# One level of Strassen's algorithm in a float32 feed-forward layer

## The chip, the core and the metric

The kernel runs on one core of one Trainium2 chip. The metric is device time in microseconds (us), from the first to the last instruction of one launch; the median of three runs before the change is 1940.48 us (1940.22 to 1940.63). The core's engines run side by side, each through its own list of instructions, and wait for each other by semaphores: TensorE (PE) multiplies, VectorE (DVE) and ScalarE (ACT) work on elements, GpSimd (POOL) does some of that and issues a few transfers, SyncE (SP) issues most transfers.

## The reference, cut to what matters

Everything is float32, with 512 tokens, a model width of 2048 and a feed-forward width of 5632:

```python
x = x + jnp.concatenate([y_f, y_g], axis=-1) @ w_out[l]      # the mixers, then the output projection
h2 = rmsnorm(x, norm_ffn[l])
x = x + (jax.nn.silu(h2 @ w_gate[l]) * (h2 @ w_up[l])) @ w_down[l]
return rmsnorm(x, norm_final)
```

The three products of the second half are what the change touches: `h2 @ w_gate` and `h2 @ w_up` (512 x 2048 times 2048 x 5632), and the down projection (512 x 5632 times 5632 x 2048).

## The kernel before, in words

**Split products.** A float32 operand is carried as two float32r tiles, hi (leading 12 bits) and lo (the rest), and a product is three matmuls: hi·hi, hi·lo and lo·hi, accumulated in PSUM (`mm3`, lines 82 to 84). Weights come from memory in units of 128 x 1024 (512 KB). ACT makes hi by a cast (line 76), DVE makes lo by a subtraction (line 77). There are three buffers each for raw, hi and lo, so a unit can be made ready while the two before it are in use.

**Stages.** Input projection and mixers (0 to about 303 us of the trace), output projection (to 485 us), feed-forward (to the end). In the output projection, four column blocks of 512 are computed one after the other; behind each block DVE adds the residual (line 459), ACT sums the squares (line 453), and PE transposes the 16 tiles of the block (line 444), from which ACT and DVE make hi and lo of the next product's operand (lines 447, 448). The norm's 1/rms by token isn't needed for that: it is applied later to the products (`ffn_scales`, lines 493 and 497).

**Feed-forward.** `gate_up(f)` computes one tile of 128 of the 5632 features, for all 512 tokens: 16 contraction tiles x 3 matmuls with 512 moving columns for the gate, as many for up, then the activation (lines 493 to 500; one multiplication by POOL, line 498). After each four such tiles (`GROUPS`), their part of the down projection is computed (`down`): 16 output tiles of 128 tokens x 512 columns, each accumulated over the four features in PSUM and then added to x by DVE (line 511). So gate, up and down alternate through the whole stage.

**What sets the order.** SP's transfers run in the order written. The other engines' instructions were put in order when the program was built, by a scheduler; each engine takes its list in that order, and an instruction that waits holds those behind it in the same list. In the trace a matmul's weight load overlaps the matmul before it.

Of the kernel before, what the change touches and what calls it, by code (L numbers as in the profile page):

```python
# [28 lines left out]
# the tile of u behind which v is ready for the gate  # L29
# [3 lines left out]
# ffn tiles per accumulation of the down projection; the last group is small, so that  # L33
# little is left to do behind the last matmul
GROUPS = [4] * 10 + [2, 2]
# [3 lines left out]
def encoder_block(ctx, tc, a, out):  # L39
    """The block on one core.  # L40

    A float32 product is carried by float32r passes: an operand is hi + lo exactly, hi its
    leading 12 bits and lo the other 12, and hi*hi + hi*lo + lo*hi is accumulated in float32.
    """
# [3 lines left out]
    # loads and stores in the order written here  # L48
# [3 lines left out]
    hpool = ctx.enter_context(tc.tile_pool(name="h", bufs=2 * KT))  # L52
    spool = ctx.enter_context(tc.tile_pool(name="s", bufs=24))
# [9 lines left out]
    def htile(name):  # L63
        return hpool.tile([P, S], F32R, tag="h", name=name)

    def weights(src, name, pieces=1):
        """A unit of weights, as hi and lo."""
        raw = wpool.tile([P, U], F32, tag="raw", name=f"raw_{name}")
        hi = wpool.tile([P, U], F32R, tag="hi", name=f"hi_{name}")
        lo = wpool.tile([P, U], F32R, tag="lo", name=f"lo_{name}")  # L70
        for i in range(pieces):
            c = slice(i * U // pieces, (i + 1) * U // pieces)
            nc.sync.dma_start(raw[:, c], src[:, c])
            if pieces > 1 and i == 0:
                nc.sync.dma_start(xrs[0][:, 1, :], a["xT"][0][:, 1, :])
            nc.scalar.copy(hi[:, c], raw[:, c])  # L76
            nc.vector.tensor_sub(lo[:, c], raw[:, c], hi[:, c])  # L77
# [12 lines left out]
    # the tensor engine's clock rises with its use: keep it at work until the first operands are there  # L90
# [9 lines left out]
    def rsqrt(dst, ssq, scale, shape, name):  # L100
        """dst = 1 / sqrt(ssq * scale + eps), with a Newton step."""
# [22 lines left out]
    def load_h(k):  # L124
# [4 lines left out]
        hi, lo = htile(f"hhi{k}"), htile(f"hlo{k}")  # L129
# [29 lines left out]
    def by_feature(ps, units, nk, rhs, name):  # L159
        """One bank: the transpose of rhs times 128 columns of weights."""  # L160
# [12 lines left out]
    def pair(name, width=U):  # L173
        """hi and lo of `width` columns."""
# [9 lines left out]
    yf = []  # mixed features, transposed, as (hi, lo)  # L184
# [15 lines left out]
    def fourier_classes(av, n, scaled):  # L200
        """The sums over the four token tiles that a DFT of 512 as 4 x 128 needs."""
# [39 lines left out]
    def fourier_features(h):  # L241
        # over the head's features, and its weights
# [7 lines left out]
        for sign, op in ((1, ALU.add), (-1, ALU.subtract)):  # L250
            # frequencies 4m+1 and their negatives
# [23 lines left out]
    def fourier_weights(n):  # L275
        """cos and sin of the head features' DFT, times the heads' weights."""
# [9 lines left out]
    def token_squares():  # L286
        """1 / rms by token, on the token's partition."""
# [25 lines left out]
    # hT is made as it is needed  # L313
# [21 lines left out]
    def gelu2(z, s, dst):  # L335
        """dst = 2 gelu(z), by tanh; s holds z squared."""
# [32 lines left out]
    # of v, where v2 = 2 v  # L369
# [10 lines left out]
    # v's place, once vn is there  # L380
# [45 lines left out]
    mix = yf + yg  # L426
    x2 = [[slot(f"x2_{m}_{i}") for i in range(2)] for m in range(NT)]

# [8 lines left out]
    h2 = []  # L437

    def transposes(n):
        for i in range(4):  # L440
            c = 4 * n + i
            ps = bank(f"xt{c}")
            for m in range(NT):
                nc.tensor.transpose(ps[:, m * P : (m + 1) * P], x2c(m, n)[:, i * P : (i + 1) * P], ident)
            hi, lo = htile(f"h2hi{c}"), htile(f"h2lo{c}")
            g = g_ffn[:, c : c + 1]
            nc.scalar.mul(hi, ps, g)
            nc.vector.scalar_tensor_tensor(lo, ps, g, hi, op0=ALU.mult, op1=ALU.subtract)
            h2.append((hi, lo))

    def squares(m, n, dst):
        j = small.tile([P, S], BF16, tag="sq", bufs=1, name=f"xsq{m}_{n}")
        nc.scalar.activation(j, x2c(m, n), AF.Square, accum_out=dst)

    for n in range(4):
        pss = [bank(f"o{n}_{m}") for m in range(NT)]
        by_token(pss, a["w_out"][n], KT, lambda k: mix[k], f"o{n}", then={4: [lambda: load_x(n)]} if n < 2 else {})
        for m in range(NT):
            nc.vector.tensor_add(x2c(m, n), pss[m], x2c(m, n))
            squares(m, n, xss[:, m, n : n + 1])  # L460
        transposes(n)
# [4 lines left out]
    rg = const.tile([P, S], F32, name="rg")  # L466
    ru = const.tile([P, S], F32, name="ru")

    def ffn_scales():
        """1 / rms by token, on every partition."""  # L470
        ps = bank("rstd2B")
        for m in range(NT):
            dg = small.tile([P, P], F32, tag="dg", name=f"dg{m}")
            nc.vector.tensor_scalar_mul(dg, ident, rstd2[:, m : m + 1])
            mm(ps[:, m * P : (m + 1) * P], ones, dg, start=True, stop=True)
        nc.vector.tensor_copy(rg, ps)
        nc.vector.tensor_scalar_mul(ru, rg, 0.5)

# [1 line left out]
    gB = [slot(f"gB{i}") for i in range(2)]  # L480
    for i in range(2):
        nc.sync.dma_start(gB[i], a["norm_final"][:, i * U : (i + 1) * U].partition_broadcast(P))
    fss = const.tile([P, NT, 4], F32, name="fss")
    act = [None] * FT

    def gate_up(f):
        pg, pu = bank(f"g{f}"), bank(f"up{f}")
        by_feature(pg, a["w_gate"][f], KT, lambda k: h2[k], f"g{f}")
        if f == 0:
            ffn_scales()  # L490
        t = slot(f"ft{f}", F32, (P, 2, S))
        z, s = t[:, 0, :], t[:, 1, :]
        nc.vector.tensor_mul(z, pg, rg)
        nc.scalar.activation(s, z, AF.Tanh, scale=0.5)
        nc.vector.scalar_tensor_tensor(z, s, 1.0, z, op0=ALU.add, op1=ALU.mult)
        by_feature(pu, a["w_up"][f], KT, lambda k: h2[k], f"up{f}")
        nc.vector.tensor_mul(s, pu, ru)
        nc.gpsimd.tensor_tensor(out=z, in0=z, in1=s, op=ALU.mult)
        act[f] = pair(f"act{f}", S)
        split(z, act[f])  # L500

    def down_units(f0, size, n):
        return [weights(a["w_down"][(f0 + 2 * j) // 2][n], f"d{f0}_{n}_{j}") for j in range(size // 2)]

    def down(f0, size, m, n, units, ps):
        for j in range(size):
            hi, lo = units[j // 2]
            c = slice((j % 2) * S, (j % 2 + 1) * S)
            t = slice(m * P, (m + 1) * P)
            mm3(ps, both(act[f0 + j], t), (hi[:, c], lo[:, c]), j == 0, j == size - 1)  # L510
        nc.vector.tensor_add(x2c(m, n), ps, x2c(m, n))  # L511

    done = 0
    f0 = 0
    for i, size in enumerate(GROUPS[:-1]):
        # a tile ahead, so that the last one's activation is not waited for
        ahead = f0 + size + 1 if i + 2 < len(GROUPS) else FT
        while done < ahead:
            gate_up(done)
            done += 1  # L520
        for n in range(4):
            units = down_units(f0, size, n)
            for m in range(NT):
                down(f0, size, m, n, units, bank(f"d{f0}_{m}_{n}"))
        f0 += size
    size = GROUPS[-1]
    fr = const.tile([P, NT], F32, name="fr")
    fs = const.tile([P, NT], F32, name="fs")
    units = []
    for n in range(4):  # L530
        raw = wpool.tile([P, U], F32, tag="raw", name=f"raw_l{n}")
        nc.sync.dma_start(raw, a["w_down"][f0 // 2][n])
        p = pair(f"dl{n}")
        split(raw, p)
        units.append([p])
    for m in range(NT):
        o = [slot(f"o{m}_{i}") for i in range(2)]
        oc = [o[n // 2][:, (n % 2) * S : (n % 2 + 1) * S] for n in range(4)]
# [90 lines left out]
```

## Time and profile before

| | |
|---|---|
| median of 3 runs | 1940.48 us |
| profiled execution: span | 1938.5 us |
| around the span | 1940.48 - 1938.5 = 2.0 us |
| PE busy | 1919.9 us (99%), 8610 matmuls |
| DVE busy | 866.2 us (45%), 1006 instructions |
| ACT busy | 544.1 us (28%) |
| feed-forward, first to last matmul | 485.3 to 1922.7 us |
| moved by DMA | 197.5 MB, 102 GB/s on the mean |

A row of the groups names the line, the engine, the operation, out<-in, the shape and the count; behind the bar stand busy time in us and the mean ns of one, then idle time ahead of it. Matmuls overlap: a row says 389 ns for one, but they start about 227 ns apart, and only the distance between starts tells the rate. PEld is the weight load of a matmul, which overlaps the matmul before it.

### The profile page before, as it was taken

How to read it: one execution, taken by the hardware profiler on the slowest of the kernel's cores; microseconds unless marked ns; L12 is line 12 of the kernel's file. 1: busy time of each engine (PE TensorE's matmuls, PEld its weight loads, DVE VectorE, ACT ScalarE, POOL GpSimd, SP SyncE). 2: the span in 40 equal slices, each digit the busy share in tenths (PEclk: the TensorE clock that was granted, in tenths of full speed). 3: DMA queues.
4: the chain of work that ended last, by engine and by line, in shares of the span. 5: the costliest groups of instructions: out<-in, count | busy, mean ns of one | idle time of the engine just before them, and what ended most of it. 6: DMA issues, size and time to landing. Idle time of an engine off the chain costs nothing.

```text
span 1938.5 us, 20697 instructions
## 1 busy us (share of the span) xinstructions
PE 1919.9 (99%) x8610; PEld 1593.7 (82%) x8610; DVE 866.2 (45%) x1006; ACT 544.1 (28%) x684; POOL 124.2 (6%) x96
## 2 busy tenths in 40 slices
PE   9999999999999999999999999999999999999996
PEld 8888888888888888888888888888888888888885
DVE  7555663333434334343444343443433433434447
ACT  6345532223322221222212222222222122222224
POOL 5001110000000000000000000000000000000003
PEclk9999999999999999999999999999999999999998
DMA  6223224423222323323233223232232232332332
GB/s 240 95 70 108 90 74 141 142 87 119 88 98 87 109 98 98 98 91 104 89 98 98 98 87 109 87 109 98 92 100 95 94 98 98 98 98 87 106 104 94
DMA packets 55965, 197.51 MB, mean 102 GB/s; under 512 B 6592, under 2 KB 6720, under 8 KB 55872
## 3 DMA queue, kind: packets, MB, share of 16 engines
q1 hardware_dynamic: 55584, 195.15, 30.2%
q8 instruction: 67, 1.10, 0.2%
q0 software_dynamic: 288, 1.05, 0.2%
q14 instruction: 26, 0.21, 0.0%
HBM read 191.98 MB, written 4.19 MB: 101 GB/s over the span
## 4 chain that ended last, share of the span: by engine, by line
PE 97%; DVE 1%; ACT 1%; DMA 0%; issue 0%; POOL 0%; SPq 0%; ACTq 0%; DVEq 0%
PE up L83 8%; PE g L82 8%; PE g L83 8%; PE up L82 8%; PE g L84 8%; PE up L84 8%; PE d L84 8%; PE d L83 8%; PE d L82 8%; PE o L84 3%; PE o L83 3%; PE o L82 3%; PE a L82 2%; PE a L83 2%; PE a L84 2%; PE v L82 1%
## 5 line engine op out<-in xcount | busy, mean ns | idle before, releaser
L82 PE MATMUL up<-h2hi,hi_up 128*128 128x512 f32 x704 | 274.0, 389 | 0.0
L83 PE MATMUL up<-h2lo,hi_up 128*128 128x512 f32 x704 | 273.9, 389 | 0.0
L82 PE MATMUL g<-h2hi,hi_g 128*128 128x512 f32 x704 | 273.9, 389 | 0.0
L84 PE MATMUL g<-h2hi,lo_g 128*128 128x512 f32 x704 | 273.9, 389 | 0.0
L83 PE MATMUL g<-h2lo,hi_g 128*128 128x512 f32 x704 | 273.9, 389 | 0.0
L84 PE MATMUL up<-h2hi,lo_up 128*128 128x512 f32 x704 | 273.9, 389 | 0.0
L82 PE MATMUL d<-hi_d,act 128*128 128x512 f32 x672 | 261.4, 389 | 0.0
L83 PE MATMUL d<-lo_d,act 128*128 128x512 f32 x672 | 261.4, 389 | 0.0
L84 PE MATMUL d<-hi_d,act 128*128 128x512 f32 x672 | 261.4, 389 | 0.0
L511 DVE TENSOR_TENSOR x<-d,x 128x512 f32<-128x512 f32 x192 | 131.4, 687 | 160.4 <-PE d L84 159.4
L77 DVE TENSOR_TENSOR lo_up<-raw_up,hi_up 128x1024 fp32r<-128x1024 f32 x88 | 141.7, 1610 | 127.8 <-ACT hi_up L76 127.8
L76 ACT CAST hi_g<-raw_g 128x1024 fp32r<-128x1024 f32 x88 | 92.8, 1054 | 367.8 <-PE g L83 144.7
L76 ACT CAST hi_d<-raw_d 128x1024 fp32r<-128x1024 f32 x84 | 88.6, 1055 | 382.2 <-PE d L84 242.8
L77 DVE TENSOR_TENSOR lo_g<-raw_g,hi_g 128x1024 fp32r<-128x1024 f32 x88 | 107.7, 1224 | 150.7 <-ACT hi_g L76 150.6
L76 ACT CAST hi_up<-raw_up 128x1024 fp32r<-128x1024 f32 x88 | 92.8, 1054 | 272.2 <-PE up L83 140.4
L77 DVE TENSOR_TENSOR lo_d<-raw_d,hi_d 128x1024 fp32r<-128x1024 f32 x84 | 114.5, 1363 | 97.3 <-ACT hi_d L76 97.3
L84 PEld LDWEIGHTS g<-h2hi,lo_g 128*128 128x128 f32 x704 | 132.1, 188 | 27.5
L82 PEld LDWEIGHTS up<-h2hi,hi_up 128*128 128x128 f32 x704 | 132.1, 188 | 27.5
L82 PEld LDWEIGHTS g<-h2hi,hi_g 128*128 128x128 f32 x704 | 132.1, 188 | 27.4
L84 PEld LDWEIGHTS up<-h2hi,lo_up 128*128 128x128 f32 x704 | 132.1, 188 | 27.4
L83 PEld LDWEIGHTS g<-h2lo,hi_g 128*128 128x128 f32 x704 | 132.1, 188 | 27.4
L83 PEld LDWEIGHTS up<-h2lo,hi_up 128*128 128x128 f32 x704 | 132.1, 188 | 27.3
(229 smaller groups left out, 2511.6 us busy)
## 6 DMA issues: line engine op xcount, KB each, us to landing
raw_g<-in_w_gate SPq DMA_DIRECT2D x88, 512.0 KB, 3.3
raw_up<-in_w_up SPq DMA_DIRECT2D x88, 512.0 KB, 3.3
raw_d<-in_w_down SPq DMA_DIRECT2D x84, 512.0 KB, 3.3
raw_o<-in_w_out SPq DMA_DIRECT2D x32, 512.0 KB, 3.3
raw_v<-in_w_v SPq DMA_DIRECT2D x16, 512.0 KB, 3.3
raw_u<-in_w_u SPq DMA_DIRECT2D x16, 512.0 KB, 3.4
raw_a<-in_w_a SPq DMA_DIRECT2D x15, 512.0 KB, 3.5
x<-in_x SPq DMA_DIRECT2D x8, 512.0 KB, 8.0
```

Of the source, the lines that this page charges most:

```text
L76: nc.scalar.copy(hi[:, c], raw[:, c])
L77: nc.vector.tensor_sub(lo[:, c], raw[:, c], hi[:, c])
L82: mm(ps, lhs[0], rhs[0], start=first, stop=False)
L83: mm(ps, lhs[0], rhs[1], start=False, stop=False)
L84: mm(ps, lhs[1], rhs[0], start=False, stop=last)
L511: nc.vector.tensor_add(x2c(m, n), ps, x2c(m, n))
```

## The change

Each of the three products is cut into 2 x 2 blocks and computed by one level of Strassen's algorithm (Winograd's form): 7 block products for 8, with sums of blocks before and after. Numbered as in the code, with A for the activations' blocks and B for the weights', the products use these operands:

- 1: A11 with B11; 2: A12 with B21; 3: A12 + t1 with B22; 4: A22 with the sum of all four B
- 5: t0 = A21 - A22 with B11 + B12; 6: t1 = t0 - A11 with B11 + B12 + B22; 7: t3 = A11 - A21 with B12 + B22

**Weights.** Of each set of four raw units (B11, B12, B22, B21) the seven forms are made by `form`: four additions of 128 x 1024 by DVE (lines 488, 489, 491, 494), then for each form a cast by ACT (line 480) and a subtraction by DVE (line 481). Raw units and sums lie in a shared pool of 43 slots of 4 KB a partition; hi and lo have three buffers each, as before. Transfers are issued four products ahead (`LEAD`).

**Order of the stages.** All 22 pairs of gate and up tiles come first, then all of down. For that the activations go to device memory (lines 598, 599, issued by POOL; four transfers of 512 KB for each pair) and come back for down (line 665, 11 x 7 transfers of 512 KB); x goes out (line 450) and comes back (line 653) too.

**Gate and up.** The blocks are 256 tokens x 256 of each 512 contraction features, so a product is 8 contraction tiles x 3 matmuls with 256 moving columns (lines 559, 563, 564; lo first): 22 pairs x 2 matrices x 7 x 24 = 7392 matmuls. Results are combined from PSUM by six operations of 128 x 256 (lines 568 to 580, two by ACT, the others by DVE). `activation` takes both matrices of a pair, makes the sums t0 to t3 of its result, and splits all eight blocks into hi and lo (lines 588 to 599), with no POOL arithmetic.

**The operand of gate and up.** The norm is now applied before the transposes (`ffn_input`): for each 512 features DVE scales x by 1/rms (line 519), PE transposes (line 525), ACT multiplies by the norm's weights (line 526), DVE makes t0 to t3 (lines 511 to 514), and ACT and DVE split all seven operands (lines 534, 535).

**Down.** Six groups of 512 x 2, 2, 2, 2, 2, 1 features, for each of two halves of the columns: 11 x 2 x 7 x 12 = 1848 matmuls with 512 moving columns (lines 690 to 692). DVE adds each product to accumulators of 128 x 2 x 512 (line 703). In the last group DVE also makes the final sums (lines 720 to 726).

```diff
-    def transposes(n):            # behind each block of the output projection
-                nc.tensor.transpose(ps[:, m * P : (m + 1) * P], x2c(m, n)[:, i * P : (i + 1) * P], ident)
+    def form(r, i, name):
+        if i == 5 and not False:
+            r[5] = slot(f"raw5_{name}")
+            nc.vector.tensor_add(r[5], r[1], r[7])
+            nc.vector.tensor_add(r[7], r[7], r[3])
+        elif i == 6:
+            nc.vector.tensor_add(r[5], r[5], r[3])
+        w = split_weights(r[5] if i in (6, 4) else r[i], f"{name}_{i}")
+        if i == 6:
+            nc.vector.tensor_add(r[5], r[5], r[2])
+        return w
...
+    def ffn_input(n):
+        xn = [slot(f"xn{n}_{i}", F32, (P, 2, S)) for i in range(2)]
         for m in range(NT):
+            nc.vector.tensor_scalar_mul(xn[m // 2][:, m % 2, :], x2c(m, n), rstd2[:, m : m + 1])
...
+        combine(t, A11, A12, A21, A22)
+        for i, s in ((1, A11), (5, t[0]), (2, A12), (6, t[1]), (7, t[3]), (3, t[2]), (4, A22)):
+            x = slot(f"hs{n}_{i}", F32R, (P, 2, 2, H))
+            nc.scalar.copy(x[:, :, 0, :], s)
+            nc.vector.tensor_sub(x[:, :, 1, :], s, x[:, :, 0, :])
...
+        def product(i, into, first=True):
+            step()
+            hi, lo = form(r, i, name)
...
+                mm(b, lo[:, c], x[:, 0, :], start=first and j == 0, stop=False, skip_group_check=True)
...
+                    mm(b, hi[:, c], x[:, 1, :], start=False, stop=False, skip_group_check=True)
+                    mm(b, hi[:, c], x[:, 0, :], start=False, stop=last, skip_group_check=True)
...
+    def activation(p, g, u):
+        s = slot(f"s{p}", F32, (P, 2, 2, H))
+        nc.scalar.activation(s, g, AF.Tanh, scale=0.5)
+        nc.vector.scalar_tensor_tensor(s, s, 1.0, g, op0=ALU.add, op1=ALU.mult)
+        nc.vector.scalar_tensor_tensor(s, s, 0.5, u, op0=ALU.mult, op1=ALU.mult)
+        t = slot(f"at{p}", F32, (P, 4, H))
+        combine([t[:, i, :] for i in range(4)], s[:, 0, 0, :], s[:, 1, 0, :], s[:, 0, 1, :], s[:, 1, 1, :])
...
+            nc.scalar.copy(hi, src)
+            nc.vector.tensor_sub(lo, src, hi)
+            nc.gpsimd.dma_start(to[:, 4 * i : 4 * i + 4, p % 2, 0, :].bitcast(F32), hi.bitcast(F32))
```

**How it moves instructions.** The first place is DVE's list around an activation. Before, the last operations of a tile stand between subtractions for units of later products; here tile 19's activation and the start of tile 20's:

```order
L497 TENSOR_TENSOR ft19_7267<-up19_7206,ru_3607 128x512
L77 TENSOR_TENSOR lo_up20_0_7404<-raw_up20_0_7402,hi_up20_0_7403 128x1024
L171 TENSOR_TENSOR act19_7333<-ft19_7267,act19_7333 128x512
L77 TENSOR_TENSOR lo_up20_1_7434<-raw_up20_1_7432,hi_up20_1_7433 128x1024
L493 TENSOR_TENSOR ft20_7398<-g20_7336,rg_3606 128x512
```

Now the same place, at the end of pair 10 and the start of pair 11 (o_up is the combined result of up, s the activation, at its sums t0 to t3, alo the lo parts; raw5, lo_gate11_5 the second form of the next gate):

```order
L578 TENSOR_TENSOR o_up10_8593<-D_up10_8631,tmp_up10_8592 128x256
L580 TENSOR_TENSOR o_up10_8593<-E_up10_8789,tmp_up10_8592 128x256
L590 SCALAR_TENSOR_TENSOR s10_8815<-s10_8815,o_up10_8593 128x1024
L511 TENSOR_TENSOR at10_8819<-s10_8815 128x256
L514 TENSOR_TENSOR at10_8819<-s10_8815 128x256
L512 TENSOR_TENSOR at10_8819<-at10_8819,s10_8815 128x256
L597 TENSOR_TENSOR alo10_0_8825<-s10_8815,ahi10_0_8824 128x1024
L513 TENSOR_TENSOR at10_8819<-at10_8819,s10_8815 128x256
L597 TENSOR_TENSOR alo10_1_8831<-at10_8819,ahi10_1_8830 128x1024
L488 TENSOR_TENSOR raw5_gate11_8868<-raw1_gate11_0_8685,raw7_gate11_0_8719 128x1024
L489 TENSOR_TENSOR raw7_gate11_0_8719<-raw7_gate11_0_8719,raw3_gate11_0_8721 128x1024
L481 TENSOR_TENSOR lo_gate11_5_8872<-raw5_gate11_8868,hi_gate11_5_8871 128x1024
```

Only the next gate's first form stands ahead of the pair's last product (its subtraction, lo_gate11_1, is one row above the first one shown); everything for its second form stands behind the whole activation.

The second place is the passage from the output projection to the feed-forward. Before, PE's list goes from the last block's transposes straight to the gate, whose other operands were made during the three blocks before:

```order
L444 MATMUL xt15_3586<-ident_89,x2_3_1_2417 128x128
L82 MATMUL g0_3613<-h2hi0_2684,hi_g0_0_3616 128x512
L83 MATMUL g0_3613<-h2lo0_2685,hi_g0_0_3616 128x512
L84 MATMUL g0_3613<-h2hi0_2684,lo_g0_0_3617 128x512
L82 MATMUL g0_3613<-h2hi1_2693,hi_g0_0_3616 128x512
```

Now all 64 transposes stand behind the last block and ahead of the gate, and DVE's list, which feeds them, goes through the four quarters of the features one after the other. Here its start (rstd2 is 1/rms of all tokens, xn the scaled x, ht the sums, hs the seven operands):

```order
L115 TENSOR_SCALAR rstd2_3445<-rsq_ffn_3446 128x4
L519 TENSOR_SCALAR xn0_0_3463<-x2_0_0_2393,rstd2_3445 128x512
L519 TENSOR_SCALAR xn0_0_3463<-x2_1_0_2395,rstd2_3445 128x512
L519 TENSOR_SCALAR xn0_1_3464<-x2_2_0_2397,rstd2_3445 128x512
L519 TENSOR_SCALAR xn0_1_3464<-x2_3_0_2399,rstd2_3445 128x512
L511 TENSOR_TENSOR ht0_0_3495<-h2_0_0_3469,h2_0_1_3470 128x512
L514 TENSOR_TENSOR ht0_1_3496<-h2_0_0_3469 128x512
L512 TENSOR_TENSOR ht0_0_3495<-ht0_0_3495,h2_0_0_3469 128x512
L513 TENSOR_TENSOR ht0_1_3496<-ht0_0_3495,h2_0_1_3470 128x512
L535 TENSOR_TENSOR hs0_1_3501<-h2_0_0_3469,hs0_1_3501 128x2x256
L535 TENSOR_TENSOR hs0_5_3504<-ht0_0_3495,hs0_5_3504 128x2x256
```

Five more rows of line 535 follow, then the same fifteen rows, from line 519 to line 535, for each of the other three quarters; the next quarter's scaling stands behind this quarter's last split, and the second form of the first gate behind the last quarter's.

More of the change, by code (lines that the diff above doesn't have):

```diff
@@ L128, in load_h @@
         xr = xrs[k // 2][:, k % 2, :]
-        hi, lo = htile(f"hhi{k}"), htile(f"hlo{k}")
+        hi, lo = pair(f"h{k}", S)
         g = g_mix[:, k : k + 1]
@@ L436, in encoder_block, with squares @@
     xss = const.tile([P, NT, 4], F32, name="xss")
-    h2 = []
-    def transposes(n):
[L440 to L453, printed above, removed]
+    def squares(src, dst, name):
+        j = small.tile([P, S], BF16, tag="sq", bufs=1, name=f"sq_{name}")
+        nc.scalar.activation(j, src, AF.Square, accum_out=dst)
     for n in range(4):
@@ L465, in encoder_block @@
     rsqrt(rstd2, xs, 1.0 / D, [P, NT], "ffn")
[L466 to L471, printed above, removed]
-        for m in range(NT):
[L473 to L477, printed above, removed]
+    hs = [dict() for _ in range(4)]
@@ new lines, in encoder_block @@
+    blocks = []
+    for p in range(FP):
+        for mat, src in gate_blocks(p):
+            blocks.append((f"{mat}{p}", (src,), (p, mat)))
+    chunk = 0
+    for gi, size in enumerate(GROUPS):
+        for np_ in range(2):
+            src = []
+            for c in range(chunk, chunk + size):
+                w = a["w_down"][c]
+                src.append((w[2 * np_][0], w[2 * np_ + 1][0], w[2 * np_][1], w[2 * np_ + 1][1]))
+            blocks.append((f"d{gi}_{np_}", src, (gi, chunk, size, np_)))
+        chunk += size
@@ new lines, in encoder_block, with step @@
+    raws = [[dict() for _ in src] for _, src, _ in blocks]
+    wanted = {}
+    for b, (name, src, _) in enumerate(blocks):
+        for i, at, places in LOADS:
+            for q, quarters in enumerate(src):
+                wanted.setdefault(b * FORMS + at, []).append((raws[b][q], i, [quarters[x] for x in places], f"{name}_{q}"))
+    LEAD = 4
+    steps = [0]
+    def step():
+        for args in wanted.pop(steps[0] + LEAD, ()):
+            load_raw(*args)
+        steps[0] += 1
+    for i in range(LEAD):
+        for args in wanted.pop(i, ()):
+            load_raw(*args)
@@ new lines, in encoder_block @@
+    for n in range(4):
+        ffn_input(n)
+    held = {}
+    for b in range(2 * FP):
+        name, _, (p, mat) = blocks[b]
+        held[mat] = matrix(raws[b][0], name)
+        if mat == "up":
+            activation(p, held.pop("gate"), held.pop("up"))
+    KINDS = ("u", "w", 11, 12, 21, 22)
+    acc = {}
+    PLACES = {11: (0, 0), 12: (0, 1), 21: (1, 0), 22: (1, 1)}
+    for np_ in range(2):
+        for k, (half, col) in PLACES.items():
+            t = acc[k, np_] = slot(f"x{k}_{np_}", F32, (P, 2, S))
+            n = 2 * np_ + col
+            for j in range(2):
+                nc.sync.dma_start(t[:, j, :], xd[2 * half + j, n // 2][:, (n % 2) * S : (n % 2 + 1) * S])
+        for k in ("u", "w"):
+            acc[k, np_] = slot(f"x{k}_{np_}", F32, (P, 2, S))
@@ L502, in down_units @@
[L502 to L513, printed above, removed]
@@ L530, in encoder_block @@
[L530 to L538, printed above, removed]
-        for n in range(4):
-            down(f0, size, m, n, units[n], bank(f"d{f0}_{m}_{n}"))
-            squares(m, n, fss[:, m, n : n + 1])
-            last = m == NT - 1 and n == 3
-            (nc.vector if last else nc.gpsimd).tensor_tensor(
-                out=oc[n], in0=x2c(m, n), in1=gB[n // 2][:, (n % 2) * S : (n % 2 + 1) * S], op=ALU.mult
-            )
+    acts = {}
@@ L546, in encoder_block @@
+    for i in ORDER:
+        load_acts(i, 0, GROUPS[0])
+    for b in range(2 * FP, len(blocks)):
+        _, _, (gi, chunk, size, np_) = blocks[b]
+        down(b)
+        if np_ == 0 and gi == len(GROUPS) - 1:
+            for i in range(2):
+                nc.sync.dma_start(gB[i], a["norm_final"][:, i * U : (i + 1) * U].partition_broadcast(P))
+    for m in (0, 1, 2, 3):
+        half, t = m // 2, m % 2
         r = fr[:, m : m + 1]
```

208 lines of the change are left out of this document (161 added, 47 removed).

## The prediction

> **What bounds the kernel now.** I read the page first, then the windows, then the timeline around single waits.
>
> ```profile
> span 1938.5 us, 20697 instructions
> PE 1919.9 (99%) x8610; PEld 1593.7 (82%) x8610; DVE 866.2 (45%) x1006; ACT 544.1 (28%) x684; POOL 124.2 (6%) x96
> PE 97%; DVE 1%; ACT 1%; DMA 0%; issue 0%; POOL 0%; SPq 0%; ACTq 0%; DVEq 0%
> 485.31:1922.70 1437.39, 1437.39 (x6347) 1.00 0.29 96
> ```
>
> PE is busy for 99% of the span and is 97% of the chain that ended last. The fourth row is the window of the feed-forward: 6336 of its 6347 matmuls are the three products', so one with 512 columns takes 1437.39 / 6347 = 0.2265 us. Nothing else is near its limit. What counts is how much shorter PE's work gets, and whether the others, now with more to do, still keep ahead of it.
>
> **PE's work.** Gate and up now move 256 columns at a time. The mixers have such matmuls, and some with 128 (start, duration):
>
> ```profile
> 104.60 0.28 PE L83 MATMUL dft<-tabs_lo,cls 128*128 128x256 f32 x1
> ...
> 105.20 0.22 PE L82 MATMUL dft<-tabs_hi,cls 128*128 128x128 f32 x1
> 238.77 0.27 PE L82 MATMUL sv<-wsps_hi,vn_hi 128*128 128x128 f32 x1
> ...
> 239.44 0.28 PE L82 MATMUL sv<-wsps_hi,vn_hi 128*128 128x128 f32 x1
> L84 PEld LDWEIGHTS g<-h2hi,lo_g 128*128 128x128 f32 x704 | 132.1, 188 | 27.5
> ```
>
> Five starts with 256 columns take 0.60 us: 0.120 each, a little over half of 0.2265. Six with 128 take 0.67: 0.112 each, so the weight loads, 188 ns by their row, follow each other every 0.112 us and don't hold 256 columns back. New work: 7392 x 0.120 = 887 us, and 1848 x 0.2265 = 418.6 for down, together 1305.6. **Removed: 1437.4 - 1305.6 = 131.8 us.** That is all the change can bring.
>
> **DVE's work.** Prices, from groups and from neighbours in the timeline:
>
> ```profile
> L77 DVE TENSOR_TENSOR lo_g<-raw_g,hi_g 128x1024 fp32r<-128x1024 f32 x88 | 107.7, 1224 | 150.7 <-ACT hi_g L76 150.6
> L511 DVE TENSOR_TENSOR x<-d,x 128x512 f32<-128x512 f32 x192 | 131.4, 687 | 160.4 <-PE d L84 159.4
> L253 DVE TENSOR_TENSOR ey<-ey,O 128x128 f32<-128x128 f32 x16 | 6.1, 379 | 0.0
> L376 DVE SCALAR_TENSOR_TENSOR vn_lo<-v,vr,vn_hi 128x1024 fp32r<-128x1024 f32 x4 | 5.0, 1279 | 1.2 <-ACT vn_hi L375 1.2
> 1008.70 1.22 DVE L77 TENSOR_TENSOR lo_d<-raw_d,hi_d 128x1024 fp32r<-128x1024 f32 x1 [1.76 <-ACT hi_d L76]
> 1009.84 0.68 DVE L511 TENSOR_TENSOR x<-d,x 128x512 f32<-128x512 f32 x1
> 489.06 0.16 DVE L112 TENSOR_TENSOR rsq_ffn<-rsq_ffn 128x4 f32<-128x4 f32 x1
> 489.25 0.16 DVE L113 TENSOR_TENSOR rsq_ffn<-rsq_ffn 128x4 f32<-128x4 f32 x1
> ```
>
> 1024 columns take 1.22 us, or 1.28 for a scalar_tensor_tensor. An independent operation starts 1.14 us after one of 1.22 (an overlap of 0.07 to 0.08), a dependent one 0.03 after its end. 256 columns aren't there: between 0.38 (128) and 0.69 (512) I take 0.45, and 0.38 behind an independent neighbour. A pair has 22 sums or subtractions of 1024 (26.4 at a mean of 1.2), ten of 256 on PSUM (4.5) and the activation (6.6): 37.5 us, against 2 x 7 x 24 x 0.120 = 40.3 on PE. So DVE's work would fit, with 7% to spare; it isn't a bound by its sum. It is one by its order.
>
> **The wait in each pair.** The order shown above puts the whole activation of a pair ahead of the next gate's second form. Three buffers of hi and lo would allow that form to be ready; the list doesn't. The handovers:
>
> ```profile
> 1902.06 0.39 PE L84 MATMUL d<-dl_hi,act 128*128 128x512 f32 x1
> 1902.49 0.69 DVE L511 TENSOR_TENSOR x<-d,x 128x512 f32<-128x512 f32 x1 [0.67 <-PE d L84]
> 496.28 1.05 ACT L76 CAST hi_g<-raw_g 128x1024 fp32r<-128x1024 f32 x1 [4.38 <-PE g L83]
> 497.36 1.23 DVE L77 TENSOR_TENSOR lo_g<-raw_g,hi_g 128x1024 fp32r<-128x1024 f32 x1
> 214.96 2.02 DVE lo_u L77
> 217.03 0.49 PE u L84
> 217.37 0.39 PE L82 MATMUL u<-hhi,hi_u 128*128 128x512 f32 x1
> ```
>
> DVE starts 0.04 us behind a matmul's recorded end, which for 256 columns is 0.28 behind its start, so 0.20 behind T, the end of its 0.120 slot. ACT to DVE costs 0.03. After a stall the second matmul starts 0.39 us behind DVE's end (216.98 to 217.37), where a slot is 0.227: a restart costs 0.16.
>
> From T, the end of the pair's last product: combine into o (0.20 to 0.65), s (to 1.96), t0 (2.44), t3 (2.82), t1 (3.20), the first lo of the activation (4.40; its cast, 1.99 to 3.04, is hidden), t2 (4.80), the second cast on ACT (4.83 to 5.88), its lo (7.13), the sum for form 5 (8.28), the sum into raw7 (9.53), lo of form 5 (10.68; its cast is hidden). PE restarts at 10.84. Meanwhile it had one product, 24 x 0.120 = 2.88 us. **It waits 8.0 us.** Between gate and up there is no activation: combine (0.65), two sums (1.80, 3.05), lo (4.20), restart 4.36: 1.5 us. I followed the rest of the pair the same way: form 2 is ready 0.9 us behind form 5, and the forms 6, 7, 3 and 4 come before PE wants them. So 21 x 8.0 + 22 x 1.5 = **201 us** (the first pair's long wait is in the next part but one). Bounds: none of it, if DVE took ready work out of order; 1 us more a pair if no neighbours overlap and a 256 costs 0.69.
>
> The transfers don't add to it: a slot that up needs latest comes free with the activation of the pair before, over 20 us ahead, and a unit lands in 3.3 us:
>
> ```profile
> raw_g<-in_w_gate SPq DMA_DIRECT2D x88, 512.0 KB, 3.3
> ```
>
> **PE's clock.** A wait of 8 us is longer than any in the feed-forward before. At both ends of the trace the clock shows what such a wait does:
>
> ```profile
> 6.35 0.80 PE L82 MATMUL a<-hi_a,hhi 128*128 128x512 f32 x1 [0.66 <-ACT hhi L131]
> ...
> 9.94 0.58 PE L84 MATMUL a<-hi_a,hlo 128*128 128x512 f32 x1
> 10.35 0.40 PE L82 MATMUL a<-hi_a,hhi 128*128 128x512 f32 x1
> 10.59 0.39 PE L83 MATMUL a<-lo_a,hhi 128*128 128x512 f32 x1
> 1922.46 0.39 PE L84 MATMUL d<-dl_hi,act 128*128 128x512 f32 x1
> 1925.20:1938.50 13.30, 0.00 (x0) 0.00 (x0) 7.13 (x17) 4.30 (x9) 2.41 (x2) 0.50 0.47 158
> ```
>
> The granted clock is 0.50 from 1925.2 on, 2.4 us behind the last matmul. At the start, matmuls of 512 columns came every 0.41 to 0.43 us for 4.0 us (6.35 to 10.35), then every 0.23. If each long wait costs 4.0 us at half the rate, it loses 2.0 us of PE: 22 x 2.0 = **44 us** (below: nothing, if the wait is too short; above: 3.4 a pair, 75).
>
> [...]
>
> **Into the feed-forward.** The norm moved ahead of the transposes, so the transposes and all operands wait for all of the output projection.
>
> ```profile
> 483.68 1.88 PE xt L444 x16
> L447 ACT ACTIVATE h2hi<-xt,g_ffn 128x512 fp32r<-128x512 f32 x16 | 10.1, 676 | 0.0
> L204 DVE TENSOR_SCALAR a0a<-a0a,rstd 128x512 f32<-128x512 f32 x2 | 0.9, 482 | 0.0
> 487.22 1.28 ACT L109 ACT_TABLE_LOAD   x1
> ```
>
> The projection's matmuls end at 483.7 - 3 x 1.9 = 478, its first three sets of transposes gone. To rstd2: the last addition (0.9), square and its sum (0.8), table load (1.3), ten short operations (1.3): 4.3 us. A quarter: four scalings (4 x 0.41), transposes behind them (0.3), four ACT multiplications (2.5), t0 to t3 (2.7), seven subtractions (7 x 0.62; their casts are hidden), 11.5 us, and four in a row since the next scaling stands behind the last subtraction: 46. Then two sums and lo of the first gate's second form: 3.7, and the restart. That product starts at 478 + 54.4 = 532.4; without a gap it would have at 485.3 + 2.9. **44 us lost** (30 if the quarters overlap on ACT, 55 if not even the casts hide).
>
> **Down, and the end.** A product of a group of two is 5.4 us; a form may be made once the third form before it is used, so it has 5.4 us, and needs 2.6 (release, cast, subtraction). DVE has 34 of 38 us a block; I followed its list through one block without a wait. Transfers: 16 units of weights and 14 of activations in 76 us, 206 GB/s, where the last figure of this row has been reached:
>
> ```profile
> 10.33:20.00 9.67, 9.67 (x44) 7.99 (x43) 9.67 (x7) 9.13 (x15) 8.28 (x6) 1.00 0.98 377
> ```
>
> Its start waits for activations (8 units of x go first, 3 us) and behind pair 21's activation on DVE (3 us): 6. The last group has one unit a form and three more sums of 1024 in each half: DVE has 27 us for PE's 19, and I count 6 us of waits. Behind the last matmul stand sixteen multiplications of 0.6 us that come after all squares: 23.6 us, 8 more than now. **Together 20 us.** ACT has half of each pair free.
>
> **The sum.** 1938.5 - 131.8 + 201 + 44 + 44 + 20 = 2115.7, and 2.0 for what lies around the span (1940.48 is the median of the runs): **2118 us**.
>
> **Rivals.** (1) PE stays the bound: the activation's chain hides, and only the two ends cost. 1938.5 - 131.8 + 44 + 20 + 2 = 1873 us. For it: DVE is at 45%, and its sum fits in a pair. Against: the list's order, with a wait at each handover. It decides where the waits, the clock's part included, stay under 68 / 22 = 3.1 us a pair, 68 being what the two ends leave of the gain. Chance 0.05. (2) The long waits are there, but too short or too well placed for the clock: 2118 - 44 = 2074. Chance 0.15. (3) POOL's four transfers of each pair, whose packets are 1 KB, disturb DVE as POOL's multiplications do now:
>
> ```profile
> L77 DVE TENSOR_TENSOR lo_up<-raw_up,hi_up 128x1024 fp32r<-128x1024 f32 x88 | 141.7, 1610 | 127.8 <-ACT hi_up L76 127.8
> ```
>
> That mean is 0.39 above the gate's 1.22, which has no POOL work beside it; 0.39 on the ten operations of the chain is 4 us a pair: 2118 + 22 x 4 = 2206. Against: POOL computes nothing in these stages. Chance 0.08. (4) The change doesn't make seven products of eight: the built list has the 9240 matmuls, so 0.01 for this and for times near the old one.
>
> **The numbers.** The forecast has 0.71; its own range, with 1 us a pair either way and the clock's bounds, is 2080 to 2165. The range for 8 in 10 goes down to take in rival 2: 2050 to 2175. This kernel's runs can't tell less than 0.2%. Faster 0.05 (rival 1), same 0.01, slower 0.94.
>
> **What would show it.** Right: in the new trace PE idle for about 8 us once a pair, ended by the subtraction of a gate's form 5, with pairs about 52 us apart; a granted clock well under 1 in that stage; one gap of some 50 us around 480 to 532; down at 0.2265 a matmul. Wrong: pairs 40 to 43 us apart, or PE waiting for transfers.

## The result: 20% slower, and 213 us more than the forecast

The changed kernel takes 2330.95 us (median; 2329.84 to 2332.14) against 1940.35 for the kernel before: a ratio of 1.2013, 95% interval 1.1996 to 1.203. The forecast was 2118 with a range of 2050 to 2175. The direction was right, the size was 213 us short.

Of the changed kernel's page, the span, the engines, TensorE's busy share in 40 slices of 58 us, and the granted clock in the same slices:

```profile
span 2330.3 us, 28178 instructions
PE 1935.3 (83%) x11506; PEld 1747.4 (75%) x11506; DVE 1470.8 (63%) x1709; ACT 802.1 (34%) x976; POOL 118.3 (5%) x133
PE   8896576799757888888778888887888889999995
PEclk9997788899979888888888888888888899999998
```

PE was busy for 99% of the span and is now busy for 83%. The slices say where: apart from single sevens and the last slice, the fives, sixes and sevens stand in slices 4 to 8 (175 to 466 us) and 11 to 13 (583 to 757 us). The first of these are the mixers, which the forecast left as they were; the second hold the passage. The windows of the changed kernel (start and end; length; PE, weight load, DVE, ACT, POOL busy with counts; granted clock, DMA share, GB/s) are, row by row, all that stands ahead of the feed-forward (input projection, mixers, output projection), the passage, gate and up, down, and the end:

```profile
0.00:622.00 622.00, 512.93 (x2202) 413.77 (x2202) 228.73 (x309) 183.44 (x265) 50.83 (x43) 0.90 0.27 92
622.00:666.00 44.00, 14.76 (x63) 12.16 (x64) 28.70 (x58) 24.23 (x44) 1.22 (x3) 0.64 0.16 58
666.00:1868.30 1202.30, 979.97 (x7394) 970.02 (x7393) 805.42 (x883) 414.21 (x471) 63.20 (x84) 0.88 0.35 120
1870.00:2308.40 438.40, 427.67 (x1848) 351.43 (x1848) 389.59 (x413) 173.27 (x182) 3.02 (x4) 0.98 0.55 193
2308.00:2330.00 22.00, 0.35 (x2) 0.00 (x0) 17.05 (x49) 6.58 (x17) 0.00 (x0) 0.62 0.51 191
```

And what PE waited for in the whole span (who, for whom: us in total, times, longest):

```profile
PE D_gate L559 <- DVE lo_gate L481: 162.7, 22, 7.5
PE u L82 <- ACT hi_u L76: 62.9, 8, 21.3
PE D_up L559 <- DVE lo_up L481: 58.7, 22, 2.8
PE xt L525 <- DVE xn L519: 29.2, 4, 8.1
PE v L82 <- ACT hi_v L76: 25.0, 3, 15.4
```

The first row is the long wait that the prediction named, 7.4 us each. The second and the fifth are in no part of the prediction. Set beside its terms (the cuts are the recorded end of the output projection's last matmul, the start of gate 0's product 5, and the recorded end of up's last matmul, at 621.96, 677.69 and 1868.27):

| stretch | predicted | measured | difference |
|---|---|---|---|
| start to the end of the output projection | 478 | 622.0 | +144 |
| from there to gate 0's product 5 | 54.4 | 55.7 | +1.3 |
| from there to the end of up: 887 - 3 of PE, 168 + 33 of waits, 44 of clock | 1129 | 1190.6 | +61.6 |
| down and the end: 418.6 + 6 + 6 + 23.6 | 454.2 | 462.0 | +7.8 |

So 144 of the 215 us of span that were missing were lost before the changed products begin, and 62 in the pairs. In the changed kernel a pair takes 54.6 us, for 51.8 in the forecast. Here is PE around both waits of one pair (start, duration; in brackets the idle time ahead and what ended it):

```profile
1027.05 0.28 PE L564 MATMUL A_up<-hs,hi_up 128*128 128x256 f32 x1
1030.00 0.57 PE L559 MATMUL D_up<-hs,lo_up 128*128 128x256 f32 x1 [2.67 <-DVE lo_up L481]
1030.37 0.42 PE L563 MATMUL D_up<-hs,hi_up 128*128 128x256 f32 x1
1030.58 0.41 PE L564 MATMUL D_up<-hs,hi_up 128*128 128x256 f32 x1
...
1033.36 0.33 PE L559 MATMUL D_up<-hs,lo_up 128*128 128x256 f32 x1
...
1051.58 0.28 PE L563 MATMUL A_gate<-hs,hi_gate 128*128 128x256 f32 x1
1051.70 0.28 PE L564 MATMUL A_gate<-hs,hi_gate 128*128 128x256 f32 x1
1059.42 0.58 PE L559 MATMUL D_gate<-hs,lo_gate 128*128 128x256 f32 x1 [7.44 <-DVE lo_gate L481]
```

At full rate 256 columns take 0.120 us (1051.58 to 1051.70). Behind a wait they come every 0.213 (from 1030.37 to 1033.36 over 14 starts), and the granted clock is 0.50 there (window 1030.4 to 1033.4). From slot end to restart the wait in up is 1030.00 - 1027.05 - 0.12 = 2.83 us, the one in gate 7.60. The half clock costs, restart included, 1.6 us there and 2.1 behind the long wait (34.8 and 47.1 us over the 22 pairs, from the distances of the 40 starts behind each wait). 336 x 0.120 = 40.3, and 40.3 + 7.6 + 2.8 + 2.1 + 1.6 = 54.4 us of 54.6: the pair is accounted for.

### The profile page after: what moved, and what is told of

The parts are those of the page before. It is cut to its first block, busy times and chain, and to the rows that moved or that the text cites. A ratio compares the mean times of both kernels' runs of the same rounds, so it can differ in the third digit from the quotient of the medians.

```text
span 2330.3 us, 28178 instructions
## 1 busy us (share of the span) xinstructions
PE 1935.3 (83%) x11506; PEld 1747.4 (75%) x11506; DVE 1470.8 (63%) x1709; ACT 802.1 (34%) x976; POOL 118.3 (5%) x133
## 5 line engine op out<-in xcount | busy, mean ns | idle before, releaser
L559 PE MATMUL D_gate<-hs,lo_gate 128*128 128x256 f32 x352 | 125.3, 356 | 162.7 <-DVE lo_gate L481 162.7
L481 DVE TENSOR_TENSOR lo_gate<-raw_gate,hi_gate 128x1024 fp32r<-128x1024 f32 x154 | 186.4, 1222 | 97.3 <-ACT hi_gate L480 97.3
L480 ACT CAST hi_gate<-raw_gate 128x1024 fp32r<-128x1024 f32 x154 | 159.1, 1047 | 207.8 <-DVE raw_gate L491 59.9
L559 PE MATMUL D_up<-hs,lo_up 128*128 128x256 f32 x352 | 120.2, 342 | 58.7 <-DVE lo_up L481 58.7
L563 PE MATMUL D_gate<-hs,hi_gate 128*128 128x256 f32 x352 | 119.7, 340 | 0.0
L564 PE MATMUL D_gate<-hs,hi_gate 128*128 128x256 f32 x352 | 119.6, 340 | 0.0
L563 PE MATMUL D_up<-hs,hi_up 128*128 128x256 f32 x352 | 113.8, 323 | 0.0
L564 PE MATMUL D_up<-hs,hi_up 128*128 128x256 f32 x352 | 113.7, 323 | 0.0
L563 PE MATMUL A_gate<-hs,hi_gate 128*128 128x256 f32 x352 | 100.0, 284 | 0.9 <-DVE hs L535 0.9
L559 PE MATMUL A_gate<-hs,lo_gate 128*128 128x256 f32 x352 | 100.1, 284 | 0.0
L564 PE MATMUL A_gate<-hs,hi_gate 128*128 128x256 f32 x352 | 99.8, 284 | 0.0
L559 PE MATMUL A_up<-hs,lo_up 128*128 128x256 f32 x352 | 99.6, 283 | 0.0
L563 PE MATMUL A_up<-hs,hi_up 128*128 128x256 f32 x352 | 99.6, 283 | 0.0
L564 PE MATMUL A_up<-hs,hi_up 128*128 128x256 f32 x352 | 99.5, 283 | 0.0
```

Of the source, the lines that this page charges most:

```text
L480: nc.scalar.copy(hi, raw)
L481: nc.vector.tensor_sub(lo, raw, hi)
L559: mm(b, lo[:, c], x[:, 0, :], start=first and j == 0, stop=False, skip_group_check=True)
L563: mm(b, hi[:, c], x[:, 1, :], start=False, stop=False, skip_group_check=True)
L564: mm(b, hi[:, c], x[:, 0, :], start=False, stop=last, skip_group_check=True)
```

## The experiments

### Where 144 us went ahead of the feed-forward

In the kernel before, SP's transfers of weights waited for three raw buffers of their own, each freed by the subtraction that reads it. Two rows of SP's waits up to 310 us, kernel before:

```profile
SPq L73 <- DVE lo_v L77: 96.6, 15, 7.9
SPq L73 <- DVE lo_u L77: 71.3, 10, 18.4
```

Now they take slots of a pool that they share with many other tiles. SP's two largest waits up to the end of the output projection, changed kernel:

```profile
SPq L73 <- ACT vt L365: 83.7, 5, 51.9
SPq L73 <- DVE yg L171: 62.4, 4, 39.7
```

One handover, at the start of u: vt is a tile of v's activation, line 365 its last reader, vn the normed v; ACT, SP and PE, from the timeline of the changed kernel:

```profile
257.08 0.18 ACT L365 ACTIVATION_READ_ACCUMULATOR vt<-v 128x1 f32 x1
257.36 9.79 SPq L73 DMA_DIRECT2D raw_u<-in_w_u  x3
269.25 4.26 ACT L375 ACTIVATE vn_hi<-v,vr 128x1024 fp32r<-128x1024 f32 x4 [1.26 <-DVE vr L371]
273.42 1.98 ACT L76 CAST hi_u<-raw_u 128x1024 fp32r<-128x1024 f32 x2
274.50 0.80 PE L82 MATMUL u<-h,hi_u 128*128 128x512 f32 x1 [21.33 <-ACT hi_u L76]
```

The first unit of u is sent for 0.1 us behind vt's last reader: it got that tile's slot. Its cast stands in ACT's list behind the whole chain of v, vn included, and PE waits for 21.3 us (the longest in the second row of PE's waits above). In the kernel before, the first cast of u stood ahead of vn (193.62 and 222.34 us). The experiment undoes this one part:

```diff
-        raw = slot(f"raw_{name}")
+        raw = wpool.tile([P, U], F32, tag="raw", name=f"raw_{name}")
...
-    spool = ctx.enter_context(tc.tile_pool(name="s", bufs=43))
+    spool = ctx.enter_context(tc.tile_pool(name="s", bufs=40))
...
-        r[i] = slot(f"raw{i}_{name}")
+        r[i] = wpool.tile([P, U], F32, tag="raw", name=f"raw{i}_{name}") if i == 1 else slot(f"raw{i}_{name}")
```

> One part of the change undone: the weight units of the first three stages get their own three raw buffers again (in the feed-forward these hold B11), and the shared pool has 40 slots for 43. Theory A, the 144 us that the output projection's end is late (622.0 for 478) are lost because raw units wait for slots of the shared pool: that end returns to 475 to 490, PE's waits for hi_u and hi_v vanish, and the time is 2331 - 144 = 2187 us (2170 to 2205). Rival, the loss comes from elsewhere (the operand h in the shared pool, or the order of the lists): the projection still ends after 600 and the time stays within 15 us of 2331.

Measured: 2187.34 us, a ratio of 1.1272 (1.1239 to 1.1304). The output projection ends at 479.4. SP's waits, and the window of the three stages, of this run:

```profile
SPq L73 <- DVE lo_v L77: 96.6, 15, 7.9
SPq L73 <- DVE lo_u L77: 71.0, 10, 18.4
...
0.00:479.50 479.50, 474.17 (x2202) 394.94 (x2202) 231.02 (x309) 184.24 (x265) 50.70 (x43) 1.00 0.37 120
```

Transfers of v and u wait for subtractions again, 25 times as in the kernel before. SP still waits, 168 us in these two rows alone; what changed is for whom: for a subtraction, at most 18.4 us, and not for a tile of another part of the stage, up to 51.9 us. PE's 2202 matmuls need 474.2 us of busy time for 512.9, with an idle time of 5.3 for 109.1: of the 142.5 us, 104 were waits, and the other 39 go with the granted clock, 1.00 for 0.90. Gate and up, at 1204 us, are as in the changed kernel. Theory A holds; the h tiles, which stayed in the shared pool, did no harm.

### The waits in a pair, and the clock

Three experiments on the changed kernel, each with the slow first stages left in. The first writes the forms of the weights one product earlier:

```diff
         def product(i, into, first=True):
             step()
-            hi, lo = form(r, i, name)
+            hi, lo = made(steps[0] - 1)
+            made(steps[0])              # the next product's form, ahead of this one's matmuls
```

> In gate and up each form is written one product earlier than its use; the activation stays where it is. Theory A, the 2.8 us wait in up comes from ScalarE's list, where form 5's cast stands behind the copy of product 1's result: both the wait and the clock loss behind it (1.6 us) go, the long wait in gate stays at 7.6 us, and the time is 2331 - 22 x 4.4 = 2234 us. Rival, VectorE's two sums are late by themselves: the wait in up stays at 2.8 and the time at 2331.

The second moves the activation:

```diff
         A = product(2, "A", False)
         nc.scalar.copy(o[:, 0, 0, :], A)
+        next(later, None)               # the pair before: tanh, s, and t0 to t3
...
         nc.vector.tensor_sub(o[:, 1, 1, :], E5, w)
+        next(later, None)               # behind product 7: the first hi and lo
...
         nc.vector.tensor_sub(o[:, 1, 0, :], E5, u)
+        next(later, None)               # behind product 3: the second hi and lo
```

> The activation of a pair is written in three pieces behind products 2, 7 and 3 of the next gate. Theory A, the long wait is the activation's place in VectorE's list: it falls to the 2.8 us that ScalarE's copy leaves, as in up, with the clock loss of up's wait (1.6 for 2.2), and the time is 2331 - 21 x 5.4 = 2218 us. Rival, VectorE has no room for the activation anywhere in a pair: as much waiting turns up behind later products, and the time stays within 20 us of 2331.

The third fills the waits:

```diff
                     mm(b, hi[:, c], x[:, 0, :], start=False, stop=last, skip_group_check=True)
+            if i == 1:
+                spare = bank(f"spare_{name}")
+                for _ in range(60 if "gate" in name else 21):
+                    mm(spare[:, :H], hi[:, :P], hs[0][1][:, 0, 0, :], start=True, stop=True)
```

> Between product 1 and product 5 PE gets matmuls that nobody reads, 60 in gate and 21 in up, 256 columns each: 7.2 and 2.5 us of the waits of 7.6 and 2.8. The lists of the other engines are unchanged. Theory A, the half clock at the restart is the price of PE's being idle: it goes, a pair takes 54.6 - 3.8 = 50.8 us, and the time is 2331 - 22 x 3.8 = 2247 us. Rival, the clock is low in this stage for another reason: the first matmuls of product 5 still come every 0.213 us, and the time stays at 2331.

Measured: 2234.39, 2233.64 and 2252.52 us, ratios of 1.1514 (1.1481 to 1.1547), 1.151 (1.1477 to 1.1544) and 1.1607 (1.1574 to 1.1641). PE's waits from about 680 us to the end of up, of the first:

```profile
PE D_gate L568 <- DVE lo_gate L481: 156.3, 21, 7.5
```

The wait in up is gone, the long one untouched: 2234 as expected. This edit moves DVE's sums as well as ACT's casts, so by itself it doesn't say which of the two was late. The changed kernel's rows do: the cause of up's wait is ACT's list. ACT and DVE at 1027 us:

```profile
1027.37 0.37 ACT L568 COPY tmp_up<-A_up 128x256 f32<-128x256 f32 x1 [7.62 <-PE A_up L564]
1027.64 1.99 ACT L480 CAST hi_up<-raw_up 128x1024 fp32r<-128x1024 f32 x2
...
1024.84 1.22 DVE L488 TENSOR_TENSOR raw_up<-raw_up,raw_up 128x1024 f32<-128x1024 f32 x1
...
1028.72 2.36 DVE L481 TENSOR_TENSOR lo_up<-raw_up,hi_up 128x1024 fp32r<-128x1024 f32 x2 [1.41 <-ACT hi_up L480]
```

ACT had been free for 7.62 us and form 5's sum (line 488) had been there since 1024.84 + 1.22 = 1026.06, but the cast stands behind the copy of product 1's result, which needs product 1's last matmul. DVE then stood idle for 1.41 us until the cast was done. So from that matmul on there is always the copy, a cast and a subtraction, 2.8 us, however early DVE is. Of the second:

```profile
PE D_up L559 <- DVE lo_up L481: 59.8, 22, 2.8
PE D_gate L559 <- DVE lo_gate L481: 56.0, 21, 2.7
PE D_gate L559 <- DVE o_gate L577: 33.6, 21, 2.9
```

The long wait fell to the 2.7 us that ACT's list leaves, as expected. The run is still 16 us slower than its forecast of 2218: a new wait of 1.6 us a pair, 33.6 in all, took the long one's place, and about half of that came back because the clock stayed up behind 15 of the 43 waits of 2.7 us (last section). Product 3 adds onto product 5's bank, which DVE must have read first (line 577), and the pieces of the activation stand ahead of that. In the changed kernel this wait isn't seen; there the scheduler had put ten of product 4's matmuls in between. Of the third:

```profile
PE D_gate L559 <- DVE lo_gate L481: 7.2, 21, 0.3
PE D_up L559 <- DVE lo_up L481: 5.4, 22, 0.2
680.00:1780.00 1100.00, 1087.38 (x8962) 1079.30 (x8961) 778.03 (x858) 397.33 (x452) 63.35 (x84) 1.00 0.37 125
```

With the useless matmuls the granted clock in the stage is 1.00 for 0.88, and 78 us (2330.95 - 2252.52) come back for 84 expected, though gate's product 5 starts no earlier (7.8 us behind product 1's last matmul, for 7.7). So the half clock is the price of PE's being idle, and not of the stage's work.

### A version with all of it

If the pool and the lists are separate causes, their cures add up. On the kernel of the first experiment (e1), the lists of PE, DVE and ACT in gate and up were then written out by hand (`PIECES`: behind which product which piece of the activation stands; `BETWEEN`: pieces put inside form 6, where DVE would wait for ACT's cast). That is e5. In e6 the passage, down and the end are written out in the same way, and the small group of down comes first:

```diff
+            for f in evac:                   # the results of product n - 1
+                f()
...
+            made(n + 2, between)             # behind the 24 matmuls of product n
...
+    PIECES = {("up", 1): [(0, 0), (6, 1)], ("gate", 6): [(3, 1)], ("gate", 7): [(4, 1)], ("gate", 4): [(5, 1)]}
+    BETWEEN = {("up", 5): [(1, 0)], ("gate", 5): [(2, 1)]}
-    ORDER = (1, 5, 2, 6, 7, 3, 4)
+    ORDER = (1, 5, 2, 6, 7, 4, 3)
```

> On the kernel of e1: in gate and up the lists of TensorE, VectorE and ScalarE are written out by hand. Each form is made two products ahead of its use, a product's results are taken out one product later, the activation is cut into seven pieces spread over the next twelve products, product 4 comes before product 3 (which adds onto product 5's bank), and transfers are issued five products ahead. Theory A, the waits in a pair were all set by order, and VectorE's 37 us fit into the 40.4 us of a pair: pairs about 41 us apart, PE without waits and without half clock in the stage, and 2187 - 22 x 13.6 = 1888 us (1880 to 1905). Rival, VectorE is so full that small waits turn up everywhere: pairs of 43 to 46 us, 1930 to 2000 us.

> e5, and three things more: in the passage the next quarter is scaled and transposed ahead of this quarter's sums and splits, with half of the scaling on ScalarE and the first two forms of the weights made before the projection ends; in down the forms are made two units ahead, and the group of one chunk comes first, not last; the end scales its first rows before the last product's results are in. Theory A: the passage falls from 55.9 to about 38 us, down from 433.7 to about 421, so 1888 - 18 - 13 = 1857 us (1845 to 1875). Rival, VectorE is the bound in down (34.4 of 38 us a block) and in the passage, so at most 10 us come back: 1878 or more.

Measured: 1885.29 us, a ratio of 0.9716 (0.9701 to 0.973), and 1905.57, 0.9819 (0.9803 to 0.9836). The window of 800 us of gate and up in the first of the two:

```profile
600.00:1400.00 800.00, 800.00 (x6669) 800.00 (x6668) 709.27 (x795) 374.95 (x417) 59.13 (x79) 1.00 0.47 157
```

From e1 to e5 302 us came back, for 299 expected. PE is busy for 800.00 of 800 us at full clock, 6669 matmuls at 0.120 us, beside a VectorE at 89%. DVE's work fits into a pair, as its sum said; only its order did not. The second of the two missed its forecast by 49 us and is 20 us slower than the first. Its passage fell to 44.4 us, for 38 expected; most of the miss is in down, 470 us for 421. PE's and DVE's largest waits in its down, and below them DVE's in the down of the first:

```profile
PE B_d L784 <- DVE lo_d L481: 7.6, 10, 0.8
PE B_d L783 <- ACT hi_d L480: 7.1, 10, 0.8
PE C_d L784 <- DVE lo_d L481: 6.1, 10, 0.8
...
DVE lo_d L481 <- ACT hi_d L480: 76.7, 70, 5.2
```

```profile
DVE lo_d L481 <- ACT hi_d L480: 46.9, 66, 4.2
```

In e5, with the scheduler's order, down took 435. PE waits at products 6 and 7 (B and C) of nearly every block, and DVE stands idle for casts 30 us longer than with the scheduler's order: in the hand-written list a sum, its cast on ACT and its subtraction follow each other with nothing of DVE's in between. The same gap inside form 6 was filled in gate and up. That this gap is the cause is read from the list and the waits; no run fills it alone. So down went back to the scheduler:

> e6 with down as in e5 (order left to the scheduler, small group last); the new passage stays. Theory A, e6's loss sits in down alone, where its hand-written order makes both units of form 6 (7.2 us on VectorE) ahead of other work and PE waits about 4 us in each block: the passage keeps its gain of 11 us, and the start of down 2 us, so 1885 - 13 = 1872 us. Rival, the passage's early forms take buffers that cost it elsewhere: no better than 1885.

```diff
-GROUPS = [2, 2, 2, 2, 2, 1]
+GROUPS = [1, 2, 2, 2, 2, 2]
```

> e7 with the group of one chunk first, not last. Theory A, the waits of 3.6 and the 2.4 us of half clock near the end of e5 come from the small group, whose units need as much of VectorE for half of PE's time: they go, 5 to 6 us less than e7: about 1867. Rival, the small group needs the same wherever it stands, and at the start VectorE is behind anyway with the last activation: the same as e7 within 2 us, or slower.

Measured: 1878.09 us, 0.9679 (0.9663 to 0.9695), and 1864.11, 0.9607 (0.9592 to 0.9621). The new passage keeps its gain (up ends at 1411.4 for 1421.2), but e7 came to 1878 and not to 1872: down starts 6.7 us behind up, where 2.9 as in e6 had been counted on (5.2 in e5). Moving the small group (e8) gained 14 us for 5 or 6 expected: down starts 2.4 us behind up, takes 431.6 us for 435.8, and behind its last matmul come 16.1 us for 22.0. That last part fits DVE's having less left over at the end; it wasn't tested by itself. The last version is 3.9% faster than the kernel before, with the same 11506 matmuls as the changed one:

```profile
span 1860.7 us, 28216 instructions
PE 1803.2 (97%) x11506; PEld 1645.2 (88%) x11506; DVE 1453.6 (78%) x1701; ACT 813.8 (44%) x984; POOL 118.4 (6%) x133
```

## Why the prediction was right and wrong

**PE's work: right.** 0.120 us a matmul of 256 columns, taken from five starts in the mixers, holds in 6669 of them in a row (800 / 6669). Of the 131.8 us that it was to bring, 117 show in the last version: PE is busy for 1803 us, for 1919.9 before.

**The step that failed: the place where the change begins.** The sum took the output projection's end from the old trace (478); it came at 622.0. That the stages ahead of the change keep their time is a term that the prediction put at nothing without a reason. It weighed slots only for the units of up ("a slot that up needs latest comes free with the activation of the pair before"), and never asked which other transfers had been moved into the pool. The diff has that line, in a helper that the stages ahead all call. The first experiment gives these 144 us back to within 1 us. It still takes 2187 us, 69 more than the forecast and above its range, so the two terms on the wait in up and the clock, below, failed in size as well. In the built lists it could have been seen as a swap of order, ACT's cast of the first unit of u behind vn; no row of the old trace could have shown it, because there the buffers were separate.

**The long wait: right in place and cause, 5% off in size.** 7.6 us for 8.0. The order of VectorE's list that the prediction went by, with the whole activation ahead of form 5, was the cause: with the activation moved, 2.7 us of the 7.4 were left.

**The wait in up: mis-sized, 2.8 for 1.5.** That is 22 x 1.3 = 29 us. The chain was followed through DVE alone, and up to the two sums it held: the second was to end 3.05 us behind the gate's last product and ended there at 3.03. I had the gate's cast "hidden" and took up's to be so too; it was the copy in ACT's list, queued for the last matmul of up's product 1, that held it.

**The clock: right at 2.1 for 2.0 a long wait, wrong in counting only those.** The sum has nothing behind up's wait of 1.5 us; at its 2.8 us it cost 34.8 us in all. In the fourth experiment, with the waits filled, the granted clock in the stage was 1.00 for 0.88, so rival 2 (no clock drop) falls. The prediction's upper bound for the clock, 3.4 us a pair (75 us), on which the upper end of its own range (2165) rests too, is a figure that no run shows: a long wait cost 2.1 us (47.1 over the 22 pairs), both waits of a pair together 3.7 (81.9). Behind up's waits of 2.7 us the clock was halved in all 22 pairs of the changed kernel, and behind 28 of 43 waits of 2.7 us in e3. The old trace had a sign that so short a wait may cost something: its clock was at 0.50 from 1925.2 us on, 2.4 us behind the last matmul.

**The passage: right.** 55.7 us for 54.4, from a sum over the rows of DVE's list for one quarter, taken four times; a quarter took 11.9 us (626.33 to 638.24, the first scaling of one to that of the next) for 11.5, and the quarters didn't overlap, as said.

**Down and the end: 8 us short.** From the end of up to down's last matmul it took 440.1 us for 430.6, and the end 22.0 for 23.6. The block of DVE's list that was followed showed no wait; PE waits 1.8 us at the start (6 had been counted), 7.4 in the first two blocks, which had been counted at nothing, and 3.3 in the small last group, with a granted clock of 0.98. In the last version, with that group first, down and the end are 14 us shorter than in e7.

**The other rivals.** Rival 3 (POOL's transfers disturb DVE) falls by one row of the groups: the gate's subtraction takes what it took before.

```profile
L481 DVE TENSOR_TENSOR lo_gate<-raw_gate,hi_gate 128x1024 fp32r<-128x1024 f32 x154 | 186.4, 1222 | 97.3 <-ACT hi_gate L480 97.3
```

Rival 1 (PE stays the bound, 1873 us) was wrong for this kernel and right about what could be had: the versions in which the waits are cured came to 1885, 1878 and 1864.

## What to carry to other kernels

When a change moves buffers into a shared pool, list every stage that allocates there, not only the stage being rewritten; SP's queue takes its transfers in the order written, and here one late slot held it for up to 51.9 us. When VectorE's or ScalarE's sum fits but its list puts a long block ahead of what TensorE wants next, cut the block into pieces, make operands two steps ahead of their use and take results out one step late: here the same arithmetic went from 1.13 (e1, the pool mended) to 0.96 of the old time. And when a wait is worked out along one engine's list, follow the lists of all engines that the operand passes through.

## What the runs showed of the hardware that was not expected

Behind 28 of the 43 waits of 2.7 us in e3 TensorE's granted clock was halved, and not always from the restart on. In the run with the moved activation (e3), one restart behind a 2.7 us wait went on at full rate, and only 1.3 us later did the matmuls fall to half, for 16 starts:

```profile
1006.26 0.39 PE L559 MATMUL D_up<-hs,lo_up 128*128 128x256 f32 x1 [2.72 <-DVE lo_up L481]
...
1007.44 0.31 PE L559 MATMUL D_up<-hs,lo_up 128*128 128x256 f32 x1
1007.56 0.41 PE L563 MATMUL D_up<-hs,hi_up 128*128 128x256 f32 x1
...
1010.96 0.29 PE L564 MATMUL A_up<-hs,hi_up 128*128 128x256 f32 x1
```

The half clock lasts from 1007.56 to 1010.96, 3.4 us. In the trace of the changed kernel each of the 127 recorded stretches of one granted clock, full or half, that end within the span lasts a whole number of times 3.41 us, from 1 to 105 times. Why that is so was not tested.

What a wait cost was not told by its length alone. Of e3's 43 waits of 2.7 us, 15 cost 0.1 us and the others 1.4 to 2.8; each of its 20 waits of 1.5 us cost 0.1. In the changed kernel the pairs come 54.6 us apart, and from 736.5 to 1852.7 us the recorded clock repeats with the same period: 20.5 us full, 3.4 half behind up's restart, 20.5 full, 10.2 half around gate's. So the 22 nearly equal losses in up (1.4 to 1.6 us) are close to one case seen 22 times. One wait's row can't give that price; the mean over a stage can (a granted clock of 0.88 here).
